# A layout turned on VectorE in place of DRAM, and a bias table written 16 times in place of 128

## The chip, the cores and the metric

The kernel runs on one core of one Trainium2 chip. The metric is the device time of one execution in microseconds (us); a figure for a kernel is the median of several executions. Engines: PE is TensorE (PEld its weight loads), DVE is VectorE, ACT is ScalarE, POOL is GpSimd, SP is SyncE, which here only issues DMAs.

## The reference

One sequence of 256 tokens of width 1024 runs in fp32 through a block (ffn1, a hybrid mixer, ffn2) and then through two layers (differential attention with an MLP, an mLSTM with an MLP). The change touches two small pieces of it.

In the mixer, each of 8 heads solves lower triangular systems of 64 rows, forward and backward in time:

```python
    a_mat = jnp.where(strict, jnp.einsum('bhnid,bhnjd->bhnij', k_beta, k) * decay, 0.0)
    a_mat = a_mat + jnp.eye(CHUNK, dtype=q.dtype)
    rhs = jnp.concatenate([v * beta[..., None], k_beta * jnp.exp(g)[..., None]], axis=-1)
    sol = lax.linalg.triangular_solve(a_mat, rhs, left_side=True, lower=True)
```

In attention, a bias is added that depends on the distance of query and key alone, one value per distance and head:

```python
        dist = (q0 + jnp.arange(Q_BLOCK))[:, None] - jnp.arange(kend)[None, :]
        bias = rel_table[t5_causal_bucket(jnp.maximum(dist, 0))]
        bias = jnp.transpose(bias, (2, 0, 1)).astype(jnp.float32)
        logits = jnp.einsum('bqhmd,bkhmd->bmhqk', qb, kb).astype(jnp.float32) * scale + bias
```

## The kernel before

**The main stream.** Every large product is done in units. A unit is 24 products of 128x128 weights with 128x256 activations: eight weight tiles, each as three products (L429, L430, L431), since fp32 weights and activations are split in a high and a low part (`whi`, `wlo`, `xh`, `xl`). Weights come as one long stream: SP issues DMAs of 1024 KB (L281, tile `raw`, three buffers), each of which feeds two units. ACT casts a unit's high part (L320, `whi`), DVE subtracts it for the low part (L323, `wlo`); this runs two units ahead of PE. PE therefore runs dry when a `raw` load lands late, or when DVE does not come round to `wlo`.

**The side work.** Everything small is written as generators in a list. `tick` steps each of them once per unit, before the unit's products are issued; a `yield` in such a generator is thus the distance of one unit, and the work after it stands one unit later in every engine's queue. All engines work strictly in the order so written. There is no planner: the place of a step is set by the count of `yield`s.

**`dn_inverse` (L1406)** is side work of the mixer's stage. It inverts the 32 diagonal blocks of 32x32 that the 64-row systems consist of on their diagonals, in place of solving row by row. The blocks are gathered as `c` (L1418 and L1424 on ACT, L1425 a transpose on DVE). The elimination (L1446, L1448: 31 steps on DVE, in groups between `yield`s) needs them as `m`, with rows and columns of each partition's 1024 elements exchanged across 32 partitions: `c` is written to DRAM (L1429) and read back by four strided DMAs (L1433). The result `x` goes the same way back: L1450 to DRAM, L1453 four reads into `xd`. Then `xt` is the transpose of `xd` (L1457 on DVE), and PE puts the 32-blocks together: 64 tiny products of 32x32 (L1464 to L1467), a copy on ACT (L1469, `t1`), 96 tiny products in one piece (L1474 to L1479), copies on POOL, DVE and ACT (L1481 to L1493), and after two more units products of 64x64 (L1503 and on).

**`bias_job` (L1009)** is side work of ffn2. One product (L1022) makes `brows`: 8 rows (one per head) of 384 distances. Attention wants them as `bias`, 128 partitions by 8 heads by 384, each partition shifted by one. A POOL DMA writes each row 128 times to DRAM (L1027, `bdram`, 1536 KB), and two POOL DMAs (L1030) read it back, their partition stride of 383 giving the shift. It is used in L1068, 145 us later.

Of the kernel before, what the change touches and what calls it, by code (L numbers as in the profile page):

```python
# [10 lines left out]
F32 = mybir.dt.float32  # L11
# [7 lines left out]
P = 128  # L19
D = 1024  # L20
S = 256
# [368 lines left out]
class Kern:  # L390
# [618 lines left out]
    def bias_job(self):  # L1009

        nc = self.nc
        es = ExitStack()
        self.bias = self.fin_attn.enter_context(self.tc.tile_pool(name="bias", bufs=1, side="right")).tile(
            [P, 8, S + P], F32, name="bias")
        keep2 = es.enter_context(self.tc.tile_pool(name="bias2", bufs=1, side="right"))
        rows = keep2.tile([8, 384], F32, name="brows")
        onehot = keep2.tile([P, 384], F32, name="onehot")
        nc.gpsimd.dma_start(onehot, self.arg["consts"][:, self.coff["onehot"][0]:])
        yield
        yield  # L1020
        ps = self.ps_up.tile([P, 384], F32, tag="up", name="up")
        nc.tensor.matmul(ps[:8], lhsT=self.vec("rel")[:33], rhs=onehot[:33], start=True, stop=True)  # L1022
        nc.scalar.copy(rows, ps[:8])
        yield

        d = self.dram.tile([8, P, 384], F32, name="bdram")
        nc.gpsimd.dma_start(d, rows.unsqueeze(1).to_broadcast([8, P, 384]))  # L1027
        yield
        for c, n in ((0, S), (P, P)):
            nc.gpsimd.dma_start(self.bias[:, :, c * 2:c * 2 + n],  # L1030
                                bass.AP(tensor=d.tensor, offset=d.offset + P - 1 + c, ap=[[383, P], [P * 384, 8], [1, n]]))
        yield
        es.close()

    def lambda_neg(self):
# [370 lines left out]
    def dn_inverse(self):  # L1406

        nc, m2, L = self.nc, self.m2, self.L
        v, t = nc.vector, nc.tensor
        four = lambda nm: m2.tile([P, 32, 32], F32, tag="inv", name=nm, bufs=3)  # L1410
        kh = lambda a: a.rearrange("p (k h) c -> p h k c", k=2)
        lf = lambda rows, cs: L[rows, :, 0:4:3, cs]
        lb = lambda rows, cs: L[rows, :, 4:6, cs]
        q = [slice(32 * s, 32 * s + 32) for s in range(4)]
        c = four("c")
        cf = m2.tile([P, 16, 32], F32, tag="inv2", name="cf", bufs=2)
        for s in range(4):
            nc.scalar.copy(kh(cf[q[s]]), lf(q[s], q[s]))  # L1418
        x = four("x")
        nc.gpsimd.memset(x, 0.0)  # L1420
        nc.gpsimd.memset(x.rearrange("p a b -> p (a b)")[:, 0:1024:33], 1.0)
        yield
        for s in range(4):
            nc.scalar.copy(kh(c[q[s], 16:]), lb(q[s], q[s]))  # L1424
        v.transpose(c[:, :16].rearrange("p a b -> p (a b)"), cf.rearrange("p a b -> p (a b)"))  # L1425
        yield
        d1 = self.dram.tile([P, 1024], F32, name="d1")
        d2 = self.dram.tile([P, 1024], F32, name="d2")
        nc.sync.dma_start(d1, c.rearrange("p a b -> p (a b)"))  # L1429
        m = four("m")  # L1430
        for s in range(4):

            nc.sync.dma_start(m[q[s]], d1[q[s]].rearrange("r (m c) -> m r c", m=32))  # L1433
        for _ in range(3):
            yield
        tmp = m2.tile([P, 256], F32, tag="tmp", name="tmp")
        done = 0
        for j in range(31):
            n, w = 31 - j, j + 1

            if done + n * w + 150 > 950:
                yield
                done = 0
            done += n * w + 150
            tt = tmp[:, :n * w].rearrange("p (a b) -> p a b", a=n)
            v.tensor_tensor(tt, m[:, j + 1:, j:j + 1].to_broadcast([P, n, w]),  # L1446
                            x[:, j:j + 1, :w].to_broadcast([P, n, w]), op=ALU.mult)
            v.tensor_sub(x[:, j + 1:, :w], x[:, j + 1:, :w], tt)  # L1448
        yield
        nc.sync.dma_start(d2, x.rearrange("p a b -> p (a b)"))  # L1450
        xd = four("xd")
        for s in range(4):
            nc.sync.dma_start(xd[q[s]], d2[q[s]].rearrange("m (r c) -> r m c", r=32))  # L1453
        for _ in range(2):
            yield
        xt = four("xt")
        v.transpose(xt.rearrange("p a b -> p (a b)"), xd.rearrange("p a b -> p (a b)"))  # L1457
        yield

        ix = lambda s, back: (s % 8, self.DIAG[s // 8 + 2 * back])  # L1460
        p = self.acc2().rearrange("p a (b c) -> p (a b) c", c=32)
        for s in range(16):
            f, b = ix(s, 0), ix(s, 1)
            t.matmul(p[q[1], s], lhsT=L[q[0], f[0], f[1], q[1]], rhs=xd[q[0], s], start=True, stop=True)  # L1464
            t.matmul(p[q[3], s], lhsT=L[q[2], f[0], f[1], q[3]], rhs=xd[q[2], s], start=True, stop=True)
            t.matmul(p[q[0], s], lhsT=L[q[1], b[0], b[1], q[0]], rhs=xt[q[1], 16 + s], start=True, stop=True)
            t.matmul(p[q[2], s], lhsT=L[q[3], b[0], b[1], q[2]], rhs=xt[q[3], 16 + s], start=True, stop=True)  # L1467
        t1 = m2.tile([P, 16, 32], F32, tag="inv2", name="t1", bufs=2)
        nc.scalar.copy(t1, p)  # L1469
        yield  # L1470
        p1 = self.acc2().rearrange("p a (b c) -> p (a b) c", c=32)
        p2 = self.acc2().rearrange("p a (b c) -> p (a b) c", c=32)
        for s in range(16):
            t.matmul(p1[q[0], s], lhsT=t1[q[1], s], rhs=xt[q[1], s], start=True, stop=True)  # L1474
            t.matmul(p1[q[2], s], lhsT=t1[q[3], s], rhs=xt[q[3], s], start=True, stop=True)
            t.matmul(p1[q[1], s], lhsT=t1[q[0], s], rhs=xd[q[0], 16 + s], start=True, stop=True)
            t.matmul(p1[q[3], s], lhsT=t1[q[2], s], rhs=xd[q[2], 16 + s], start=True, stop=True)
            t.matmul(p2[q[1], s], lhsT=xt[q[1], s], rhs=t1[q[1], s], start=True, stop=True)
            t.matmul(p2[q[2], s], lhsT=xd[q[2], 16 + s], rhs=t1[q[2], s], start=True, stop=True)  # L1479
        for s in range(4):  # L1480
            nc.gpsimd.tensor_copy(lf(q[s], q[s]), kh(xt[q[s], :16]))  # L1481
            nc.gpsimd.tensor_copy(lb(q[s], q[s]), kh(xd[q[s], 16:]))
        x64 = m2.tile([P, 16, 64], F32, tag="inv", name="x64", bufs=3)
        lo, hi = slice(0, 32), slice(32, 64)
        nc.vector.memset(x64, 0.0)
        for r, cc, src in ((0, lo, xd[q[0], :16]), (1, hi, xd[q[1], :16]), (2, lo, xt[q[2], 16:]), (3, hi, xt[q[3], 16:])):
            v.tensor_copy(x64[q[r], :, cc], src)
        v.tensor_scalar(x64[q[1], :, lo], p2[q[1]], -1.0, None, op0=ALU.mult)
        v.tensor_scalar(x64[q[2], :, hi], p2[q[2]], -1.0, None, op0=ALU.mult)
        nc.scalar.mul(lf(q[0], q[1]), kh(p1[q[0]]), -1.0)  # L1490
        nc.scalar.mul(lf(q[2], q[3]), kh(p1[q[2]]), -1.0)
        nc.scalar.mul(lb(q[1], q[0]), kh(p1[q[1]]), -1.0)
        nc.scalar.mul(lb(q[3], q[2]), kh(p1[q[3]]), -1.0)  # L1493
        yield
        yield

        u, w = slice(0, 64), slice(64, 128)
        t2 = m2.tile([P, 16, 64], F32, tag="inv", name="t2", bufs=3)
        for g in range(2):
            p = self.acc2().rearrange("p a (b c) -> p (a b) c", c=64)  # L1500
            for h in range(8):
                s = 8 * g + h
                t.matmul(p[w, h], lhsT=L[u, h, self.DIAG[g], w], rhs=x64[u, s], start=True, stop=True)  # L1503
                t.matmul(p[u, h], lhsT=L[w, h, self.DIAG[2 + g], u], rhs=x64[w, s], start=True, stop=True)
            nc.scalar.copy(t2[:, 8 * g:8 * g + 8], p)
        yield
        for g in range(2):
            f, b = self.DIAG[g], self.DIAG[2 + g]
            p = self.acc2().rearrange("p a (b c) -> p (a b) c", c=64)
            for h in range(8):  # L1510
                s = 8 * g + h
                t.matmul(p[u, h], lhsT=t2[w, s], rhs=L[w, h, f, w], start=True, stop=True)
                t.matmul(p[w, h], lhsT=t2[u, s], rhs=L[u, h, b, u], start=True, stop=True)
            nc.scalar.mul(L[u, :, f, w], p[u], -1.0)
            nc.scalar.mul(L[w, :, b, u], p[w], -1.0)
        yield
# [763 lines left out]
```

## Time and profile before

| what | value |
|---|---|
| time, median of 3 runs | 1355.5 us (1355.3 to 1356.18) |
| the profiled execution | 1354.97 us, its span 1353.2 us |
| mean granted clock of PE | 0.983 of full |
| PE busy | 1311.7 us, 97% of the span |
| DVE / ACT / POOL busy | 967.1 (71%) / 662.0 (49%) / 51.0 (4%) us |
| DMA moved | 259.99 MB, mean 192 GB/s |

The profiled execution lies 0.5 us below the median. PE's share is an average: it is busy nearly all the time, so what a change can bring lies in the few places where it is not, or where it runs at the lower of its clock levels (a product of 128x256 starts every 0.12 us at the full one, every 0.21 us at the half one). A matmul's own duration in the rows is longer than this distance, since successive ones overlap. In a row of the timeline, the brackets say how long the engine was idle before the instruction and what ended it.

### The profile page before, as it was taken

What the parts mean: (1) busy time and instruction counts of PE and PEld (TensorE: products, weight loads), DVE (VectorE), ACT (ScalarE), POOL (GpSimd) and SP (SyncE); (2) the same over time, 40 slices, a digit from 0 to 9 for tenths busy, and PEclk for the clock granted to TensorE, in tenths of its full rate; (3) what the DMA queues carried; (4) which work ended last, traced back from release to release, by engine and by line L of the source; (5) the groups of instructions that cost most, each with busy time, mean ns of one, the idle gap of its engine ahead of it and who ended that gap; (6) DMA issues with size and microseconds to landing.
All of it is one profiled execution on the core that took longest, in us unless ns stands there. A gap on an engine that the chain in (4) does not pass through costs nothing.

```text
span 1353.2 us, 26491 instructions
## 1 busy us (share of the span) xinstructions
PE 1311.7 (97%) x11090; PEld 1293.7 (96%) x11090; DVE 967.1 (71%) x1830; ACT 662.0 (49%) x1044; POOL 51.0 (4%) x36
## 2 busy tenths in 40 slices
PE   8999999999989999978999999999999999999997
PEld 7999999999979999978999999999999999999997
DVE  7997768789985587936446886876666957966664
ACT  3544445668434355614445555544444664644442
POOL 0000000343010000000000000000000000000000
PEclk8999999999989999988999999999999999999998
DMA  9898853444554365578554443455554435455550
GB/s 368 339 366 320 302 226 129 145 168 171 172 187 157 118 226 171 196 187 293 187 187 156 156 156 125 165 194 184 186 180 161 156 127 185 160 186 186 187 187 32
DMA packets 45912, 259.99 MB, mean 192 GB/s; under 512 B 12888, under 2 KB 13144, under 8 KB 15328
## 3 DMA queue, kind: packets, MB, share of 16 engines
q1 hardware_dynamic: 43744, 253.57, 53.3%
q0 software_dynamic: 1184, 3.35, 1.3%
q8 instruction: 87, 1.43, 0.4%
q10 hardware_dynamic: 864, 1.38, 0.3%
q14 instruction: 33, 0.27, 0.1%
HBM read 254.60 MB, written 3.67 MB: 191 GB/s over the span
## 4 chain that ended last, share of the span: by engine, by line
PE 84%; DVE 9%; DMA 3%; ACT 2%; issue 1%; SPq 0%; DVEq 0%; ACTq 0%
PE up L429 16%; PE up L431 15%; PE up L430 15%; PE acc L430 9%; PE acc L429 9%; PE acc L431 9%; DVE wlo L323 2%; DMA raw<-in_stream 2%; DVE raw L553 2%; PE acc L466 1%; PE acc L470 1%; PE acc L1297 1%; PE acc L1562 1%; PE acc L467 1%; PE acc L699 1%
## 5 line engine op out<-in xcount | busy, mean ns | idle before, releaser
L320 ACT CAST whi<-raw 128x1024 fp32r<-128x1024 f32 x404 | 420.4, 1047 | 434.7 <-PE up L430 166.5
L323 DVE TENSOR_TENSOR wlo<-raw,whi 128x1024 fp32r<-128x1024 f32 x389 | 472.5, 1223 | 79.4 <-ACT whi L320 77.5
L429 PE MATMUL up<-xh,whi 128*128 128x256 f32 x1744 | 503.5, 289 | 10.1 <-ACT whi L320 10.1
L431 PE MATMUL up<-xh,wlo 128*128 128x256 f32 x1744 | 497.9, 285 | 2.8 <-DVE wlo L323 2.8
L430 PE MATMUL up<-xl,whi 128*128 128x256 f32 x1744 | 497.3, 285 | 0.0
L429 PEld LDWEIGHTS up<-xh,whi 128*128 128x128 f32 x1744 | 338.8, 194 | 11.8 <-ACT whi L320 10.5
L431 PEld LDWEIGHTS up<-xh,wlo 128*128 128x128 f32 x1744 | 337.8, 194 | 4.5 <-DVE wlo L323 4.3
L430 PEld LDWEIGHTS up<-xl,whi 128*128 128x128 f32 x1744 | 337.9, 194 | 0.6 <-DVE xl L758 0.2
L429 PE MATMUL acc<-gh,whi 128*128 128x256 f32 x864 | 244.2, 283 | 0.0
L431 PE MATMUL acc<-gh,wlo 128*128 128x256 f32 x864 | 244.2, 283 | 0.0
L430 PE MATMUL acc<-gl,whi 128*128 128x256 f32 x864 | 244.1, 283 | 0.0
L429 PEld LDWEIGHTS acc<-gh,whi 128*128 128x128 f32 x864 | 166.0, 192 | 0.6 <-issue 0.6
L431 PEld LDWEIGHTS acc<-gh,wlo 128*128 128x128 f32 x864 | 164.7, 191 | 0.0
L430 PEld LDWEIGHTS acc<-gl,whi 128*128 128x128 f32 x864 | 164.7, 191 | 0.0
L991 DVE TENSOR_TENSOR t<-up,rs 128x256 f32<-128x256 f32 x60 | 25.4, 423 | 101.9 <-PE up L431 101.9
L553 DVE SCALAR_TENSOR_TENSOR raw<-raw,crow 128x1024 f32<-128x1024 f32 x72 | 85.7, 1218 | 3.3 <-DMA raw<-in_stream 3.3
L917 DVE TENSOR_TENSOR gf<-up,sa 128x256 f32<-128x256 f32 x35 | 14.5, 422 | 69.2 <-PE up L431 69.2
L323 POOL TENSOR_TENSOR wlo<-raw,whi 128x1024 fp32r<-128x1024 f32 x15 | 36.2, 2417 | 282.5 <-ACT whi L320 282.5
L429 PE MATMUL up<-whi,xh 128*128 128x256 f32 x128 | 37.3, 291 | 0.2 <-DVE raw L1933 0.2
L429 PE MATMUL acc<-yh,whi 128*128 128x256 f32 x128 | 36.3, 284 | 0.0
L913 ACT ACTIVATE sa<-up 128x256 f32<-128x256 f32 x35 | 13.2, 382 | 47.1 <-PE up L431 43.5
L430 PE MATMUL up<-wlo,xh 128*128 128x256 f32 x128 | 36.1, 282 | 0.0
(485 smaller groups left out, 1827.1 us busy)
## 6 DMA issues: line engine op xcount, KB each, us to landing
raw<-in_stream SPq DMA_DIRECT2D x238, 1024.0 KB, 5.0
bdram<-brows POOLq DMA_DIRECT2D x1, 1536.0 KB, 37.2
h<-in_x SPq DMA_DIRECT2D x2, 512.0 KB, 4.5
bias<-bdram POOLq DMA_DIRECT2D x1, 1024.0 KB, 10.4
d<-c SPq DMA_DIRECT2D x1, 512.0 KB, 2.6
m<-d SPq DMA_DIRECT2D x4, 128.0 KB, 4.0
d<-x SPq DMA_DIRECT2D x1, 512.0 KB, 5.6
xd<-d SPq DMA_DIRECT2D x4, 128.0 KB, 3.6
```

Source lines behind the costliest of these rows:

```text
L320: nc.scalar.copy(hi[:, :n], raw)
L323: self.lows.append(lambda: eng.tensor_tensor(lo[:, :n], raw, hi[:, :n].bitcast(F32), op=ALU.subtract))
L429: t.matmul(ps, lhsT=wh, rhs=xh, start=start, stop=False, skip_group_check=True)
L430: t.matmul(ps, lhsT=wh, rhs=xl, start=False, stop=False, skip_group_check=True)
L431: t.matmul(ps, lhsT=wl, rhs=xh, start=False, stop=stop, skip_group_check=True)
L466: t.matmul(ps, lhsT=wh[:, s], rhs=x[0][:, k], start=k == 0, stop=False, skip_group_check=True)
L467: t.matmul(ps, lhsT=wl[:, s], rhs=x[0][:, k], start=False, stop=False, skip_group_check=True)
L470: t.matmul(ps, lhsT=wh[:, s], rhs=x[1][:, k], start=False, stop=k == KT - 1, skip_group_check=True)
L553: self.nc.vector.scalar_tensor_tensor(w, w, 1.0, self.crow, op0=ALU.mult, op1=ALU.mult, accum_out=self.mods[:, c:c + 1])
L699: self.nc.tensor.matmul(ps[:, c0 + b * P:c0 + (b + 1) * P], lhsT=tok[:, b:b + 1].to_broadcast([P, P]), rhs=self.const("ident"), start=True ...
L917: product(n, lambda gf: None, lambda gf: nc.vector.tensor_tensor(gf, ps, sa, op=ALU.mult))
L991: nc.vector.tensor_tensor(t, src, self.rs, op=ALU.mult)
```

## The change

Three edits.

1. In `dn_inverse` the two trips through DRAM go (two writes and eight reads on SP's queue). In their place DVE transposes 32x32 blocks with strided views: `m` from `c` and `xd` from `x`, each of 128x1024 elements. The three `yield`s behind the first trip become one, the two behind the second become one; the limit that closes a group of elimination steps goes from 950 to 900, which makes 14 groups of 13.
2. The 96 tiny products are cut in two halves of 48 by a `yield`, so that a unit's 24 products stand between them.
3. In `bias_job` each row goes to DRAM 16 times in place of 128 (192 KB). Eight reads of 16 partitions each (128 KB), two per `yield`, make `bias[:, :, :256]`; three `yield`s later POOL copies the last 128 columns, which equal columns 128 to 255.

```diff
-        d = self.dram.tile([8, P, 384], F32, name="bdram")
-        nc.gpsimd.dma_start(d, rows.unsqueeze(1).to_broadcast([8, P, 384]))
-        yield
-        for c, n in ((0, S), (P, P)):
-            nc.gpsimd.dma_start(self.bias[:, :, c * 2:c * 2 + n],
-                                bass.AP(tensor=d.tensor, offset=d.offset + P - 1 + c, ap=[[383, P], [P * 384, 8], [1, n]]))
-        yield
+        d = self.dram.tile([8, 16, 384], F32, name="bdram")
+        nc.gpsimd.dma_start(d, rows.unsqueeze(1).to_broadcast([8, 16, 384]))
+        yield
+        for q in range(0, P, 16):
+            nc.gpsimd.dma_start(self.bias[q:q + 16, :, :S],
+                                bass.AP(tensor=d.tensor, offset=d.offset + P - 1 - q, ap=[[383, 16], [16 * 384, 8], [1, S]]))
+            if q % 32:
+                yield
+        for _ in range(3):
+            yield
+        nc.gpsimd.tensor_copy(self.bias[:, :, S:], self.bias[:, :, P:S])
         es.close()
...
-        d1 = self.dram.tile([P, 1024], F32, name="d1")
-        d2 = self.dram.tile([P, 1024], F32, name="d2")
-        nc.sync.dma_start(d1, c.rearrange("p a b -> p (a b)"))
         m = four("m")
-        for s in range(4):
-
-            nc.sync.dma_start(m[q[s]], d1[q[s]].rearrange("r (m c) -> m r c", m=32))
-        for _ in range(3):
-            yield
+
+        v.transpose(m.rearrange("p r c -> p c r"), c.rearrange("p m c -> p c m"))
+        yield
...
-            if done + n * w + 150 > 950:
+            if done + n * w + 150 > 900:
...
-        nc.sync.dma_start(d2, x.rearrange("p a b -> p (a b)"))
         xd = four("xd")
-        for s in range(4):
-            nc.sync.dma_start(xd[q[s]], d2[q[s]].rearrange("m (r c) -> r m c", r=32))
-        for _ in range(2):
-            yield
+        v.transpose(xd.rearrange("p m c -> p c m"), x.rearrange("p r c -> p c r"))
+        yield
...
             t.matmul(p2[q[2], s], lhsT=xd[q[2], 16 + s], rhs=t1[q[2], s], start=True, stop=True)
+            if s == 7:
+                yield
```

Counting `yield`s from the transpose of `c` to the first tiny product gives 20 before and 18 after: this product stands two units earlier in PE's queue.

On DVE, at the end of the inverse, the queue reads so before (from the last elimination step; `ct`, `cy`, `cb`, `yal` are the convolution branch of the mixer, `wlo` the stream):

```order
L1446 TENSOR_TENSOR tmp<-m,x 128x31
L1448 TENSOR_TENSOR x<-x,tmp 128x31
L323 TENSOR_TENSOR wlo<-raw,whi 128x1024
L1738 SCALAR_TENSOR_TENSOR cy<-ct,vecs,cy 128x255
L1740 SCALAR_TENSOR_TENSOR cy<-ct,vecs,cy 128x255
L1742 TENSOR_TENSOR cb<-cb,cy 128x256
L323 TENSOR_TENSOR wlo<-raw,whi 128x1024
L1734 TENSOR_TENSOR ct<-up,cc 128x256
L323 TENSOR_TENSOR wlo<-raw,whi 128x1024
L489 TENSOR_TENSOR yal<-cb,yah 128x256
L1457 STREAM_TRANSPOSE xt<-xd 128x1024
```

And so after, from the same step (line numbers are those of the changed kernel; L1445 and L1447 are the elimination, L1450 the new transpose, L1453 the old one):

```order
L1445 TENSOR_TENSOR tmp<-m,x 128x31
L1447 TENSOR_TENSOR x<-x,tmp 128x31
L1732 TENSOR_TENSOR ct<-up,cc 128x256
L323 TENSOR_TENSOR wlo<-raw,whi 128x1024
L489 TENSOR_TENSOR yal<-cb,yah 128x256
L1450 STREAM_TRANSPOSE xd<-x 128x32x32
L323 TENSOR_TENSOR wlo<-raw,whi 128x1024
L1736 SCALAR_TENSOR_TENSOR cy<-ct,vecs,cy 128x255
L1738 SCALAR_TENSOR_TENSOR cy<-ct,vecs,cy 128x255
L1740 TENSOR_TENSOR cb<-cb,cy 128x256
L1453 STREAM_TRANSPOSE xt<-xd 128x1024
```

The elimination ends earlier against the stream's work (the first `ct`, `wlo`, `yal` now come behind it), and the transpose to `xt` stands directly behind the convolution's `cb`, where two more `wlo` stood ahead of it before.

On PE, the middle of the second group of tiny products before, at the place where half of them are issued:

```order
L1478 MATMUL acc<-t_4882,xt 32x32
L1479 MATMUL acc<-t_4882,xd 32x32
L1474 MATMUL acc<-xt,t_4882 32x32
L1475 MATMUL acc<-xt,t_4882 32x32
L1476 MATMUL acc<-xd,t_4882 32x32
L1477 MATMUL acc<-xd,t_4882 32x32
```

And the same place after (L1474 and L1475 are the last two of the first half):

```order
L1474 MATMUL acc<-t_4802,xt 32x32
L1475 MATMUL acc<-t_4802,xd 32x32
L429 MATMUL up<-xh,whi 128x256
L430 MATMUL up<-xl,whi 128x256
L431 MATMUL up<-xh,wlo 128x256
```

A whole unit of 24 products follows there, and the other 48 tiny products come behind it.

On POOL, around the bias table before (the onehot table's load first, the next stage's first work last):

```order
L1018 DMA onehot<-in_consts 128x384
L1027 DMA bdram<-brows 1024x1x384
L1030 DMA bias<-bdram 128x8x256
L1030 DMA bias<-bdram 128x8x128
L1885 TENSOR_TENSOR sq<-sq 128x2x256 x2
```

And after:

```order
L1018 DMA onehot<-in_consts 128x384
L1027 DMA bdram<-brows 128x1x384
L1030 DMA bias<-bdram 16x8x256 x8
L1036 COPY bias<-bias 128x8x128
L1883 TENSOR_TENSOR sq<-sq 128x2x256 x2
```

The write is an eighth of what it was, the reads are eight small ones, and one copy takes the place of the second read; nothing else of POOL's moves.

## Rows read from the trace of the kernel before

**Rows 1.** the chain that ended last, shares of the span by engine (page)

```profile
PE 84%; DVE 9%; DMA 3%; ACT 2%; issue 1%; SPq 0%; DVEq 0%; ACTq 0%
```

**Rows 2.** PE's waits over the run: waited for, total us, times, longest

```profile
PE up L429 <- ACT whi L320: 10.1, 2, 6.3
...
PE acc L1465 <- DMA xd<-d: 1.9, 1, 1.9
```

**Rows 3.** PE's timeline in the mixer: start us, us, instruction [idle before]

```profile
393.47 0.28 PE L430 MATMUL up<-xl,whi 128*128 128x256 f32 x1
393.59 0.28 PE L431 MATMUL up<-xh,wlo 128*128 128x256 f32 x1
...
399.43 0.26 PE L1466 MATMUL acc<-xt,L 32*32 32x32 f32 x1 [1.71 <-DVE xt L1457]
...
401.28 0.58 PE L429 MATMUL up<-xh,whi 128*128 128x256 f32 x1
...
406.14 0.28 PE L431 MATMUL up<-xh,wlo 128*128 128x256 f32 x1
...
410.49 0.21 PE L1476 MATMUL acc<-xd,t 32*32 32x32 f32 x1 [2.39 <-issue]
```

**Rows 4.** two windows there; PEclk is third from the right

```profile
400.00:405.00 5.00, 5.00 (x117) 4.94 (x107) 4.77 (x6) 0.58 (x1) 4.92 (x6) 0.50 0.65 223
...
410.00:415.00 5.00, 4.51 (x43) 4.47 (x44) 2.45 (x4) 3.57 (x6) 0.00 (x0) 1.00 0.02 3
```

**Rows 5.** DVE's timeline from the first `wlo` behind `c` to `xt`

```profile
336.44 0.41 DVE L1302 TENSOR_TENSOR Pm<-acc,Pm 128x256 f32<-128x256 f32 x1
...
343.61 1.23 DVE L323 TENSOR_TENSOR wlo<-raw,whi 128x1024 fp32r<-128x1024 f32 x1 [1.96 <-ACT whi L320]
...
347.05 0.20 DVE L1446 TENSOR_TENSOR tmp<-m,x 128x31 f32<-128x31 f32 x1
...
386.48 0.19 DVE L1446 TENSOR_TENSOR tmp<-m,x 128x31 f32<-128x31 f32 x1
...
388.98 0.43 DVE L1742 TENSOR_TENSOR cb<-cb,cy 128x256 f32<-128x256 f32 x1
...
398.13 1.25 DVE L1457 STREAM_TRANSPOSE xt<-xd 128x1024 f32<-128x1024 f32 x1 [5.14 <-DMA xd<-d]
```

**Rows 6.** PE's timeline in ffn2

```profile
594.05 0.28 PE L431 MATMUL acc<-gh,wlo 128*128 128x256 f32 x1
600.64 0.58 PE L429 MATMUL up<-xh,whi 128*128 128x256 f32 x1 [6.32 <-ACT whi L320]
...
613.82 0.39 PE L429 MATMUL up<-xh,whi 128*128 128x256 f32 x1 [3.81 <-ACT whi L320]
...
620.97 0.28 PE L431 MATMUL up<-xh,wlo 128*128 128x256 f32 x1
```

**Rows 7.** DMA issues: KB each, median us to landing (page)

```profile
raw<-in_stream SPq DMA_DIRECT2D x238, 1024.0 KB, 5.0
bdram<-brows POOLq DMA_DIRECT2D x1, 1536.0 KB, 37.2
...
bias<-bdram POOLq DMA_DIRECT2D x1, 1024.0 KB, 10.4
...
m<-d SPq DMA_DIRECT2D x4, 128.0 KB, 4.0
```

**Rows 8.** POOL's timeline in ffn2

```profile
574.80 1.11 POOL L1027 DMA_DIRECT2D bdram<-brows  x1 [8.85 <-ACT brows L1023]
```

**Rows 9.** DMA, 585 to 590 us: queue shares of 16 engines, issues

```profile
q0 software_dynamic: 52, 0.24, 48.0%
...
raw<-in_stream SPq DMA_DIRECT2D x1, 1024.0 KB, 25.8
```

**Rows 10.** DMA, 615 to 620 us: queue shares, issues

```profile
raw<-in_stream SPq DMA_DIRECT2D x2, 1024.0 KB, 8.5
```

**Rows 11.** POOL on 128x1024: busy us, mean ns of one (page)

```profile
L323 POOL TENSOR_TENSOR wlo<-raw,whi 128x1024 fp32r<-128x1024 f32 x15 | 36.2, 2417 | 282.5 <-ACT whi L320 282.5
```

## The prediction

> **What bounds the kernel now.** I read the chain of waits first: 84% of it is PE [rows 1], so time is lost where PE waits or runs slowly, and almost nowhere else. The list of PE's waits then gives the places. The largest entry, 10.1 us in two waits for ACT's casts of weights, is in ffn2. A wait of 1.9 us for `xd`, the inverse's second trip through DRAM, stands in the mixer [rows 2]. Last I read the timelines of PE around both places. In the mixer PE's last product starts at 393.59 and the first group of tiny products, after a wait for `xt` of 1.71 us more, gets going at 399.43; the unit behind it crawls from 401.28 to 406.14; and in the middle of the 96 tiny products PE sits 2.39 us with nothing to wait for that the profile shows ("issue") [rows 3]. In ffn2 PE stands for 6.32 and 3.81 us, and the products between run at the wide distance [rows 6].
>
> **The bias table.** The write of 1536 KB takes 37.2 us to land [rows 7]. While it runs, its queue holds 48.0% of the 16 engines' time though it moves only 0.24 MB in 5 us, and a weight load takes 25.8 us in place of 5.0 [rows 7, 9]. The write is issued at 574.8 [rows 8]; the raw buffers cover it up to PE's last product at 594.05, 19.25 us [rows 6]; then ACT has nothing to cast and PE stands. What this costs comes from the first and the last of the disturbed products: from 594.05 to 620.97 there are 78 of them, which at full speed need 78 x 0.12 = 9.36 us, so 26.92 - 9.36 = 17.56 us are lost [rows 3, 6]. Of these 10.13 are the two waits; most of the rest is PE at half clock behind them.
>
> The change writes an eighth. At the same rate that is 37.2 / 8 = 4.65 us, a quarter of the stretch that the buffers cover. If it takes twice that, the cover still holds. The eight reads are bounded from below by the reads of before: 1536 KB in two DMAs, 10.4 us for the larger [rows 7], beside which weight loads took 8.5 us [rows 10]. A load feeds two units, 48 products or 5.76 us, and three are in flight, so 8.5 us starve nobody. From above, the nearest row of this size is `m<-d`, 128 KB in 4.0 us [rows 7]: two reads in one unit's time are then no more traffic than before, spread over four units. I take the whole loss as gone but for half a microsecond: gain 17.0, between 14 (one late load left) and 17.56. POOL's copy of 128x1024 elements costs at most 2.4 us by its subtraction of that size [rows 11]; PE and ACT do not wait for it, as attention needs the table over 100 us later. That distance covers the longer `bias_job` as well.
>
> **The inverse: what DVE now carries.** The trips through DRAM leave SP's queue, where weight loads stood behind them; two transposes go to DVE. Before, DVE worked from 336.44 nearly without a gap: one wait of 1.96 us at 343.61, and at 389.33 its last `cb` is done (start 388.98 plus 0.35 until the next instruction) [rows 5]. That is 52.9 - 1.96 = 50.9 us of work. The new order puts the same work ahead of `xt`, plus the two transposes of T us each; since the elimination starts two units earlier, its first steps fill that gap. So `xt` starts at 336.44 + 50.9 + 2T = 387.3 + 2T.
>
> T is not in the trace. Contiguous, a transpose of 128x1024 takes 1.25 us [rows 5]; from below there is no reason for less. For strided access the elimination shows something: its first step walks 31 elements 128 bytes apart and takes 0.20 us, its last 31 side by side in 0.19 [rows 5]. If the 0.01 us is all due to the stride it makes 0.33 us per 1024, so T = 1.6; if the whole 0.20 grew with the elements, T = 6.6, the far end. I take 1.25 to 1.6, since the row says that the stride costs next to nothing, and sum with 1.25.
>
> [...]
>
> With T = 1.25 `xt` starts at 389.8, ends at 391.05, and tiny products start at 391.1. Before they started at 399.43, but two units (2 x 2.88 = 5.76 us) later in PE's order: 393.67 on the same footing. Gain 2.55. PE itself would be there at 393.71 - 5.76 = 387.95, so a wait of about 3 us stays, and DVE is what PE waits for; part of it will show as late `wlo` in the units ahead.
>
> **Clock.** Behind these waits the granted clock is 0.50 [rows 4], the lower of the two levels, and the unit takes 4.86 us, where 23 distances of 0.12 are 2.76: 2.1 lost [rows 3]. Behind the pause of 2.39 us the clock is 1.00 [rows 3, 4]; behind one of 3.81 PE crawls again (620.97 - 613.82 is 7.15 us) [rows 6]. A wait of 3 us in two or three pieces lies nearer the first. I take the 2.1 as gained; the other end is 0.
>
> **The halves.** The 2.39 us pause [rows 3] comes after most of the 96 tiny products, each with its own weight load, have gone in one run, and nothing that the profile shows is waited for: I read it as PE running out of fetched instructions. With 48 products, then a unit of 2.9 us, then 48, I expect the pause to go; gain 2.4, or 0 if the supply needs longer. The 64x64 products behind stand no nearer to the last tiny ones than before, so no wait is added there.
>
> **Sum.** Inverse 2.55 + 2.1 + 2.4 = 7.05, bias 17.0, together 24.0. On the profiled execution: 1354.97 - 24.0 = 1331.0; it lies 0.5 below the median of the runs, so by the median 1331.5. I say 1331. The main case's own range goes down to 1325.5: 17.56, with 5.7 + 2.1 + 2.4 in the mixer if PE never stands there, makes 1327.2, and 1.7 more are for clock and waits elsewhere. It goes up to 1334, where the pause is kept.
>
> **Rivals.**
> 1. DVE becomes the bound in the inverse. With T = 2.5, twice the contiguous row, `xt` starts at 392.3, PE at 393.6, the gain there is nothing, PE stands 5.6 us and the clock falls as before: the mixer gives 2.4 or nothing. Time 1354.97 - 17.0 - 2.4 = 1335.6, or 1338 with the pause kept. At T = 6.6 PE starts at 401.8, 8.1 us are lost there, and the time is 1344 to 1346. For it: DVE had one gap of 1.96 us in this stretch of 53. Against: the 0.20 beside 0.19. Chance 0.18.
> 2. The narrow reads hold the engines as the write did. At the write's rate (1536 KB in 37.2 us, 41 KB/us) 1024 KB last 24.8 us, 29.4 with the write. Of the write's 37.2 us the last 17.9, behind the cover of 19.25, carried the loss of 17.56; 29.4 leave 10.2 us behind the cover, so 10 us of loss: gain 7.6 in place of 17.0, time 1340.3. For it: the rate fits a transfer with 8 partitions on one side, and these reads have 16. Against: `m<-d`, 32 partitions wide, does 128 KB in 4.0 us [rows 7]. Chance 0.10. [...]
> 3. The slower side: each small read takes as long as the large one, 10.4 us, one after the other, with weight loads at 25.8 us all the while. That is 83 + 4.65 us, 68.6 behind the cover; at 17.56 lost per 17.9 us it costs 67 us in place of 17.56, so 1354.97 + 49.5 - 7.05 = 1397. It eats up the mixer's gain from 44 us in all, 5.0 us per read in a row. For it: the reads go out on the queue that delayed the loads. Against: beside the reads of before loads took 8.5 us, not 25.8 [rows 10]. Chance 0.04.
> 4. The write does not shrink: it still reads 8 partitions, and if a fixed part, not the bytes, makes its 37.2 us, then only the mixer's 7.05 are left: 1348. Chance 0.04.
>
> **Chances and range.** The main case has 0.64. A measurement of this kernel can tell about 0.2%, 2.7 us. All cases but the third are faster by more: 0.95 faster, 0.01 the same, 0.04 slower. From 1325.5 to 1341 the range takes in the main case, rival 1 up to T near 5, and rival 2; left out are 3, 4 and the tails.
>
> **What would show it.** Right: the waits for `xd` gone and the one at the first tiny product for DVE's transpose, 3 us or less, at most 4 with the `wlo` before it; strided transposes of 1.2 to 1.6 us; granted clock near 1.00 from 395 to 410; no "issue" wait in either half; `bdram` landing in 4 to 8 us; weight loads under 10 us in ffn2; no wait of PE for a cast there. Wrong: a strided transpose above 2 us; a pause in the tiny products still there; weight loads over 15 us beside the eight reads; or a new place at which PE stands for POOL or DVE in ffn2.

## The result, and the profile after

The changed kernel takes 1339.5 us (median; 1337.6 to 1340.4), the kernel before 1355.4 on the same chip: a ratio of 0.9883, 95% interval 0.9866 to 0.9901. That is 16 us less, faster as forecast, but two thirds of the 24 us that the sum gave (1331). It lies in the stated range of 1325.5 to 1341, but above the 1334 at which the main case's own part of it ends.

To see where the time went I lined the two traces up product by product: both have 9456 products of the main stream (L429 to L431), and the n-th of one is the n-th of the other. The difference of their start times, before less after, in us:

```
product                          before at   difference
2304  ahead of the inverse          325.4        0.25
3048  behind the mixer's solve      476.6        6.36
3900  ahead of the disturbed ffn2   587.0        6.54
4200  behind it                     640.4       16.10
9432  end                          1337.3       15.78
```

So the mixer gives 6.1 (7.05 forecast) and ffn2 gives 9.7 (17.0 forecast). Nearly all of the missing time is in ffn2.

PE's waits of the changed kernel (waited for: total us, times, longest) answer to [rows 2]:

```profile
PE up L429 <- ACT whi L320: 5.0, 1, 5.0
...
PE acc L1462 <- DVE xt L1453: 2.5, 1, 2.5
...
PE acc L1301 <- ACT V L1396: 1.1, 1, 1.1
```

The waits for `xd` are gone, and one of 2.5 us for DVE's transpose stands in their place. One of the two waits for casts in ffn2 is still there, with 5.0 us. A small new one, 1.1 us for `V`, at 339.6 us, stands in every kernel that has the edits to the inverse and in neither of the two without them. DVE's timeline after, which answers to [rows 5]:

```profile
336.20 2.13 DVE L1433 STREAM_TRANSPOSE m<-c 128x1024 f32<-128x1024 f32 x1
...
386.66 2.25 DVE L1450 STREAM_TRANSPOSE xd<-x 128x1024 f32<-128x1024 f32 x1
...
391.27 1.24 DVE L1453 STREAM_TRANSPOSE xt<-xd 128x1024 f32<-128x1024 f32 x1
```

The strided transposes take 2.13 and 2.25 us, near the first rival's 2.5 and not the 1.25 of the sum. Hence `xt` comes at 392.5, and on PE (to compare with [rows 3]):

```profile
389.91 0.19 PE L1461 MATMUL acc<-xd,L 32*32 32x32 f32 x1
392.57 0.26 PE L1462 MATMUL acc<-xt,L 32*32 32x32 f32 x1 [2.46 <-DVE xt L1453]
...
394.41 0.58 PE L429 MATMUL up<-xh,whi 128*128 128x256 f32 x1
...
395.63 0.28 PE L431 MATMUL up<-xh,wlo 128*128 128x256 f32 x1
...
397.77 0.28 PE L431 MATMUL up<-xh,wlo 128*128 128x256 f32 x1
```

The unit behind crawls for five products only (394.41 to 395.63), then runs at full distance; it takes 3.36 us, not 4.86. No "issue" row appears. The granted clock (third from the right) in windows after, the first behind the new wait for `V`, the others behind that for `xt`:

```profile
340.00:345.00 5.00, 5.00 (x29) 4.92 (x28) 4.73 (x15) 0.05 (x2) 0.00 (x0) 0.66 0.65 210
...
390.00:395.00 5.00, 2.54 (x130) 2.37 (x127) 3.55 (x5) 2.15 (x4) 2.31 (x3) 0.72 0.25 66
395.00:400.00 5.00, 5.00 (x128) 4.83 (x128) 1.84 (x4) 1.57 (x3) 3.18 (x6) 0.94 0.48 197
```

Behind the wait for `xt` it is 0.72 and 0.94, where before it fell to 0.50 [rows 4]; from 340 to 345 us it is 0.66, where the kernel before had 1.00.

In ffn2, POOL's timeline (the write, the eight reads, the copy) and PE's, to compare with [rows 6, 8]:

```profile
570.49 0.63 POOL L1027 DMA_DIRECT2D bdram<-brows  x1 [11.06 <-ACT brows L1023]
576.41 4.20 POOL L1030 DMA_DIRECT2D bias<-bdram  x8 [5.29 <-DMA bdram<-brows]
596.96 1.04 POOL L1036 COPY bias<-bias 128x1024 f32<-128x1024 f32 x1 [16.35 <-DMA bias<-bdram]
```

```profile
593.22 0.28 PE L431 MATMUL up<-xh,wlo 128*128 128x256 f32 x1
598.50 0.58 PE L429 MATMUL up<-xh,whi 128*128 128x256 f32 x1 [5.00 <-ACT whi L320]
...
603.90 0.29 PE L429 MATMUL up<-xh,whi 128*128 128x256 f32 x1
```

The write lands within 5.9 us: it has shrunk as forecast. But the reads last from 576.4 to 597.0, twenty microseconds for 1 MB, and at their end PE stands. From 593.22 to 603.90 there are 22 products, so 10.68 - 22 x 0.12 = 8.0 us are lost; 17.56 - 8.0 = 9.5 is what ffn2 gained, near the 9.7 of the lined-up traces.

Two windows show the difference between the old reads and the new. The DMA of the kernel before while its wide reads ran, 612 to 627 us (queue: packets, MB, share of the 16 engines; then the issues):

```profile
q1 hardware_dynamic: 532, 3.88, 65.0%
q0 software_dynamic: 416, 1.57, 31.3%
...
raw<-in_stream SPq DMA_DIRECT2D x3, 1024.0 KB, 8.5
```

And of the changed kernel while its narrow reads run, 577 to 598 us:

```profile
q1 hardware_dynamic: 510, 3.74, 75.1%
q0 software_dynamic: 384, 1.05, 24.6%
...
raw<-in_stream SPq DMA_DIRECT2D x4, 1024.0 KB, 13.5
bias<-bdram POOLq DMA_DIRECT2D x7, 128.0 KB, 11.9
```

The engines are full in both, but the weights (q1) get 3.88 MB in 65.0% of 16 x 15 us, 24.9 KB per engine and us, before, and 3.74 MB in 75.1% of 16 x 21, 14.8 KB, after. While the narrow reads are about, the weight packets are slow as well (0.54 us for one of 8 KB, median, in place of 0.31), and a weight load takes 13.5 us where it took 8.5.

### The profile page after: what moved, and what is told of

Its sections match the earlier page's. It is cut to its first block, busy times and chain, and to the rows that moved or that the text cites. A ratio compares the mean times of both kernels' runs of the same rounds, so it can differ in the third digit from the quotient of the medians.

```text
span 1337.5 us, 26486 instructions
## 1 busy us (share of the span) xinstructions
PE 1305.4 (98%) x11090; PEld 1288.1 (96%) x11090; DVE 969.2 (72%) x1832; ACT 661.3 (49%) x1044; POOL 52.4 (4%) x43
## 3 DMA queue, kind: packets, MB, share of 16 engines
HBM read 253.03 MB, written 1.25 MB: 190 GB/s over the span
## 4 chain that ended last, share of the span: by engine, by line
PE 86%; DVE 9%; DMA 2%; ACT 2%; issue 1%; SPq 0%; DVEq 0%; ACTq 0%
PE up L429 16%; PE up L431 16%; PE up L430 16%; PE acc L430 9%; PE acc L429 9%; PE acc L431 9%; DVE wlo L323 2%; DVE raw L553 2%; DMA raw<-in_stream 1%; PE acc L699 1%; PE acc L1301 1%; PE acc L1560 1%; PE acc L466 1%; PE acc L470 1%; PE acc L467 1%
## 5 line engine op out<-in xcount | busy, mean ns | idle before, releaser
L429 PE MATMUL up<-xh,whi 128*128 128x256 f32 x1744 | 501.5, 288 | 5.0 <-ACT whi L320 5.0
L431 PE MATMUL up<-xh,wlo 128*128 128x256 f32 x1744 | 495.4, 284 | 1.8 <-DVE wlo L323 1.8
L429 PEld LDWEIGHTS up<-xh,whi 128*128 128x128 f32 x1744 | 336.9, 193 | 6.5 <-ACT whi L320 5.2
L431 PEld LDWEIGHTS up<-xh,wlo 128*128 128x128 f32 x1744 | 335.6, 192 | 2.9 <-DVE wlo L323 2.7
L429 PE MATMUL acc<-gh,whi 128*128 128x256 f32 x864 | 244.3, 283 | 0.0
L431 PE MATMUL acc<-gh,wlo 128*128 128x256 f32 x864 | 244.3, 283 | 0.0
L429 PEld LDWEIGHTS acc<-gh,whi 128*128 128x128 f32 x864 | 166.1, 192 | 0.6 <-issue 0.6
L431 PEld LDWEIGHTS acc<-gh,wlo 128*128 128x128 f32 x864 | 164.7, 191 | 0.0
L429 PE MATMUL up<-whi,xh 128*128 128x256 f32 x128 | 37.3, 292 | 0.2 <-DVE raw L1931 0.2
L429 PE MATMUL acc<-yh,whi 128*128 128x256 f32 x128 | 36.3, 284 | 0.0
```

Source lines behind the costliest of these rows:

```text
L429: t.matmul(ps, lhsT=wh, rhs=xh, start=start, stop=False, skip_group_check=True)
L431: t.matmul(ps, lhsT=wl, rhs=xh, start=False, stop=stop, skip_group_check=True)
```

## The experiments

All times are medians; ratios are to the kernel before on the same chip.

| run | time | ratio, 95% interval | mixer, ffn2 (lined up, us gained) |
|---|---|---|---|
| changed kernel | 1339.5 | 0.9883 (0.9866 to 0.9901) | 6.1, 9.7 |
| bias_alone | 1344.9 | 0.9922 (0.9903 to 0.9941) | 0.1, 10.1 |
| inverse_alone | 1350.3 | 0.9963 (0.9948 to 0.9977) | 3.4, 1.7 |
| comb_reads | 1335.4 | 0.9848 (0.9832 to 0.9863) | 4.8, 15.5 |
| transpose_prices | 1340.8 | one run | 4.2, 10.2 |
| reads_on_sp | 1333.7 | 0.9832 (0.9813 to 0.9850) | 4.2, 17.5 |
| rows_128 | 1362.1 | one run | 4.1, -9.1 |
| heads_128 | 1350.2 | one run | 4.8, -0.3 |
| no_cut | 1342.0 | one run | 4.5, 9.0 |
| one_unit_more | 1339.5 | 0.9873 (0.9859 to 0.9888) | 4.9, 9.6 |
| xt_early | 1332.9 | 0.9812 (0.9791 to 0.9832) | 5.6, 16.5 |
| three_cuts | 1330.9 | 0.9811 (0.9791 to 0.9832) | 7.6, 16.7 |

The last column is of one profiled execution each, products 2304 to 3048 and 3048 to 4200. It carries some 1.5 us that I take for chance: in the solve behind the inverse the granted clock falls for a few us in most of these executions, at changing places (455 to 460 us: 0.66 in comb_reads; 465 to 470: 0.77 before), and in those of the changed kernel and of bias_alone it does not. That it is chance is not shown, since each kernel has one trace; the mean clock of one kernel's executions does differ, 0.986 to 0.988 in the changed kernel.

**Do the parts add up?** bias_alone puts the third edit of the diff into the kernel before; inverse_alone leaves it out of the changed one.

> The kernel before with the bias edit alone. Lined up product by product, the changed kernel's traces give 9.4 us to ffn2 and 6.1 to the mixer. Theory: the two parts do not touch each other, so this kernel is 9.4 us faster than before: about 1346. The eight reads land in about 11 us each and weight loads beside them in 13 to 16, with one wait of PE for a cast of about 5 us. Rival: the weight loads of ffn2 are late only because the shorter mixer shifts them against the reads; then this kernel has no such wait and is 16 to 17 us faster, about 1339.

> The kernel before with the edits to the inverse alone (transposes, 900, the two halves). Theory, parts independent: 6.1 us faster than before, about 1349, with the strided transposes at 2.1 to 2.3 us, a wait of 2.5 us for the transpose to xt, no pause in the tiny products, and ffn2 losing the 17.6 us of before. Rival: the mixer's gain is taken back in ffn2, where the long write starves PE by the weights' place in the queue; then less than 3 us faster.

They gave 10.6 us (1 - 0.9922 of 1355) and 5.0 us, together 15.6 against 15.9 for both. Each of these is good to 2 or 3 us; as far as that shows, the parts do not touch each other, and the rivals fall. bias_alone's waits and inverse_alone's:

```profile
PE up L429 <- ACT whi L320: 3.9, 2, 3.7
...
PE acc L1480 <- issue: 2.5, 1, 2.5
```

```profile
PE up L429 <- ACT whi L320: 9.7, 2, 6.1
...
PE acc L1458 <- DVE xt L1449: 2.5, 1, 2.5
```

With the bias edit alone the wait for a cast remains (3.9), and the pause of the inverse as well; with the inverse alone the 9.7 of the long write remain.

**Neighbours or the source?** The eight reads of the changed kernel, with the partitions of each 8 apart (`comb[q]` is partitions q, q + 8, ..., q + 120 of `bias`):

```diff
-            nc.gpsimd.dma_start(self.bias[q:q + 16, :, :S],
-                                bass.AP(tensor=d.tensor, offset=d.offset + P - 1 - q, ap=[[383, 16], [16 * 384, 8], [1, S]]))
+            nc.gpsimd.dma_start(comb[q, :, :, :S],
+                                bass.AP(tensor=d.tensor, offset=d.offset + P - 1 - q, ap=[[376, 16], [16 * 384, 8], [1, S]]))
```

> The changed kernel, but each of the eight reads fills 16 partitions that lie 8 apart in place of 16 neighbours; same write, same 16 rows of DRAM, same bytes, count and places of the DMAs. Theory N: 16 neighbouring partitions are what is slow; spread over all 128, the reads land in 3 to 6 us, weight loads beside them in under 9, PE does not wait for a cast, and the time falls by about 7.7 us to 1332. Rival S: the source (16 rows of 1.5 KB read by eight DMAs) or the small DMAs themselves are slow; then reads stay near 11 us, the wait of 5 us stays and the time is 1339 to 1340.

In between. PE's wait for the cast fell from 5.0 to 1.0 us, and the time to 1335.4; but the reads land in 9.6 us, not 3 to 6. The weights' queue in the window 577 to 590:

```profile
q1 hardware_dynamic: 319, 2.35, 65.3%
```

The weights get 2.35 MB in 65.3% of 16 x 13 us, 17.3 KB per engine and us: between 14.8 and 24.9. So which partitions a read fills matters, with source and size the same; it is not all.

**Distinct rows, then whole width.** rows_128 writes each row 128 times again and gives the narrow reads the distinct rows that the wide reads had; heads_128 reads the same bytes in eight DMAs of the same 128 KB, but each over all 128 partitions for one head.

```diff
 rows_128:
...
+            nc.gpsimd.dma_start(self.bias[q:q + 16, :, :S],
+                                bass.AP(tensor=d.tensor, offset=d.offset + P - 1 + 383 * q, ap=[[383, 16], [P * 384, 8], [1, S]]))
 heads_128:
...
+            nc.gpsimd.dma_start(self.bias[:, q, :S],
+                                bass.AP(tensor=d.tensor, offset=d.offset + P - 1 + P * 384 * q, ap=[[383, P], [1, S]]))
```

> The changed kernel, but each row is written 128 times as before and the eight reads of 16 neighbouring partitions take distinct rows, as the wide reads of before did. The long write costs its 17 us again, so the time is about 1350; what counts is the stretch of the reads. Theory S (16 rows shared by all reads are the slow source): reads land in under 8 us and the weight loads beside them in about 8.5, as beside the wide reads of before. Theory D (the small narrow DMAs themselves are slow): reads stay at 10 us or more, and loads beside them at 11 to 15.

> As rows_128 (each row written 128 times, eight reads of 128 KB, two per unit, on POOL's queue), but each read fills all 128 partitions for one head, in place of 16 partitions for eight heads. Theory W (what is slow is that a read fills few partitions): reads land in under 8 us, weight loads beside them in about 8.5, and the third wait of PE for a cast, 4.8 us in rows_128, is gone; time 1352 to 1354. Theory C (eight small reads are slow by their count and size): reads stay over 10 us, loads at 11 or more, the third wait stays, time about 1362.

The stretch of the reads in rows_128, 609 to 629 us, and in heads_128, 609 to 620:

```profile
q1 hardware_dynamic: 440, 3.23, 66.4%
q0 software_dynamic: 375, 1.03, 35.1%
...
raw<-in_stream SPq DMA_DIRECT2D x3, 1024.0 KB, 13.8
bias<-bdram POOLq DMA_DIRECT2D x8, 128.0 KB, 16.8
```

```profile
q1 hardware_dynamic: 388, 2.85, 66.5%
q0 software_dynamic: 384, 1.05, 31.0%
...
raw<-in_stream SPq DMA_DIRECT2D x3, 1024.0 KB, 6.7
bias<-bdram POOLq DMA_DIRECT2D x8, 128.0 KB, 6.0
```

This settles it between the source and the width. With distinct rows the narrow reads are no better (16.8 us, worse even), so the 16 shared rows were not the fault. With the same source, bytes, count and queue, only the width differs between the two, and with it which rows one DMA takes: 4.26 MB in 20 us against 3.90 MB in 11, and for the weights 15.2 KB per engine and us against 24.4. PE's waits for casts, of rows_128 and then heads_128:

```profile
PE up L429 <- ACT whi L320: 16.1, 3, 7.6
```

```profile
PE up L429 <- ACT whi L320: 12.4, 2, 8.3
```

The third is gone, and the time is 12 us lower, in single runs; 8.8 of the 12 lie in ffn2. (rows_128 was expected at about 1350, and missed that by 12.) So a read on this queue that fills 16 partitions holds the engines, and the weights with them: these got 14.8 KB per engine and us beside 16 neighbours, 17.3 beside the comb, 24.4 beside 128. Why this is so, and why the comb costs less than neighbours, no run shows. In the changed kernel, beside the weight loads, 1.05 MB took the 20.6 us from the first issue to POOL's copy, 51 GB/s, and no run shows the reads alone.

**Another queue.** reads_on_sp issues the same narrow reads from SP, between the weight loads, three units after the write.

```diff
+        for _ in range(3):
+            yield
         for q in range(0, P, 16):
-            nc.gpsimd.dma_start(self.bias[q:q + 16, :, :S],
+            nc.sync.dma_start(self.bias[q:q + 16, :, :S],
```

> The changed kernel with its eight reads issued by SP, in the weights' own queue, three units after the write. Theory Q (two queues that take turns on the same 16 engines are slow): each read lands in 3 to 5 us as m<-d did, weight loads near them in under 8, no wait of PE for a cast, time 1331 to 1333. Theory S (these 16 rows are a slow source, whoever asks): reads and the loads behind them stay slow, at 10 us or more, a wait of some us stays, time 1336 to 1340.

1333.7 us, and no wait of PE for a cast in the whole run: ffn2 gave 17.5, all of the 17.56. Window 577 to 598 (the reads are on q1 here):

```profile
q1 hardware_dynamic: 1504, 5.75, 93.8%
...
raw<-in_stream SPq DMA_DIRECT2D x5, 1024.0 KB, 8.0
bias<-bdram SPq DMA_DIRECT2D x8, 128.0 KB, 9.9
```

The time is near what theory Q had, the landing is not: a read takes 9.9 us from issue, not 3 to 5; it shares its queue with five weight loads. What is gained is that one after the other they move 5.75 MB in 21 us, where two queues at once moved 4.79 (3.74 + 1.05). Narrow reads still cost, but they no longer slow the weight packets beside them: a weight packet of 8 KB takes 0.31 us here (median), as beside the wide reads of before, and 0.54 in the changed kernel's window. With the queue the edit changed two things more, the reads' packets (1 KB in place of 4) and their time (three units later); no run parts these from the queue.

**The price of a stride.** transpose_prices adds eight transposes on a scratch tile:

```diff
+        for ki, ko in ((1, 1), (2, 1), (4, 1), (32, 1), (1, 2), (1, 4), (1, 32), (32, 32)):
+            nc.vector.transpose(tb.rearrange("p (a b) -> p b a", b=ko), ta.rearrange("p (a b) -> p b a", b=ki))
+            yield
```

> The changed kernel with eight transposes of 128x1024 added in ffn2, one per unit, on a scratch tile: reading with a step of 1, 2, 4 and 32 elements and writing side by side, then writing with a step of 2, 4 and 32, then 32 on both sides. Theory L (a price for every element that lies on another 16-byte line): step 2 as step 1 (1.25 us), steps 4 and 32 alike and dearer, near 2.2. Theory B: only the strided writing, or only both together, is dear; then three or more of the strided forms stay at 1.25 and the last is 2.2. By either the time is a few us above the changed kernel's.

In that order (reading steps 1, 2, 4, 32 elements; writing steps 2, 4, 32; both 32):

```profile
610.62 1.24 DVE L1043 STREAM_TRANSPOSE pb<-pa 128x1024 f32<-128x1024 f32 x1
...
613.22 1.23 DVE L1043 STREAM_TRANSPOSE pb<-pa 128x1024 f32<-128x1024 f32 x1
...
615.81 2.09 DVE L1043 STREAM_TRANSPOSE pb<-pa 128x1024 f32<-128x1024 f32 x1
...
618.92 2.09 DVE L1043 STREAM_TRANSPOSE pb<-pa 128x1024 f32<-128x1024 f32 x1
...
622.03 1.25 DVE L1043 STREAM_TRANSPOSE pb<-pa 128x1024 f32<-128x1024 f32 x1
...
624.62 2.07 DVE L1043 STREAM_TRANSPOSE pb<-pa 128x1024 f32<-128x1024 f32 x1
...
627.97 2.07 DVE L1043 STREAM_TRANSPOSE pb<-pa 128x1024 f32<-128x1024 f32 x1
...
631.33 2.24 DVE L1043 STREAM_TRANSPOSE pb<-pa 128x1024 f32<-128x1024 f32 x1
```

The prices are as theory L had them: a step of 2 (8 bytes) is free (1.23 us reading, 1.25 writing, beside 1.24), 4 (16 bytes) costs 0.85 us, 32 no more than 4, reading or writing alike (2.09 and 2.07 us), and both together only 0.15 more (2.24). Of the reason that theory L gives, a line of 16 bytes, the run shows no more than that the price comes between steps of 8 and of 16 bytes. Both sides of the kernel's own transposes are strided, by 32 elements, and they took 2.13 and 2.25 us.

**The pause in the tiny products.** no_cut takes the `yield` between the two halves out; one_unit_more puts one more `yield` behind the transpose to `xt`.

```diff
 no_cut:
-            if s == 7:
-                yield
 one_unit_more:
         v.transpose(xt.rearrange("p a b -> p (a b)"), xd.rearrange("p a b -> p (a b)"))
         yield
+        yield
```

> The changed kernel without the yield that cuts the 96 tiny products. Theory I (PE runs out of fetched instructions when 96 products with their loads go in one run): a pause of 2 to 2.5 us before one of the last products comes back, nothing else moves, time 1341 to 1342. Rival: the pause of before was an after-effect of the waits on DRAM; then no pause, and the time is that of the changed kernel.

> The changed kernel with one more yield behind the transpose to xt, so that PE does a unit of 2.9 us there. Theory: DVE's lateness at this one place is all that PE waits for; the wait of 2.5 us and the half clock behind it go, 3 to 3.7 us in all, and the time is 1336. Rival: DVE is the bound of the whole stretch; then the wait shows up again at a wlo or at the 64x64 products, and the time stays within 1 us of the changed kernel.

Theory I, as it was put, falls. In no_cut the 96 products go in one run without a pause; its mixer gains 4.5 us, as much as the kernels that share the rest of it (4.1 to 4.8 in comb_reads, rows_128 and heads_128). Its 1342.0, a single run, lies in the range of theory I, but not by a pause. And one_unit_more, with the cut in place, has a pause:

```profile
PE acc L1473 <- issue: 1.7, 1, 1.7
```

Its wait for `xt` is gone as expected, but the pause and the clock that falls behind it (0.75 from 405 to 410 us) take the gain back: 1339.5, as before the edit. So the cut is not what removed the pause.

The traces show what did. On the page of the kernel before, PE's records and the queue of instructions:

```profile
PE 1311.7 (97%) x11090; PEld 1293.7 (96%) x11090; DVE 967.1 (71%) x1830; ACT 662.0 (49%) x1044; POOL 51.0 (4%) x36
...
q8 instruction: 87, 1.43, 0.4%
```

Its 87 packets of 16 KB go with PE's 22180 records (weight loads and products), 255 to a packet. Counted from the start of the run, every pause lies ahead of record 6811, or of record 6299, which is 2 x 256 earlier, and ends 1.3 to 1.5 us after a packet of this queue has landed:

| kernel | pause ahead of record | packet, from and to (us) | PE goes on (us) |
|---|---|---|---|
| before | 6811 | 407.86, 409.17 | 410.49 |
| bias_alone | 6811 | 407.80, 408.72 | 410.21 |
| one_unit_more | 6811 | 401.62, 402.56 | 403.81 |
| xt_early (below) | 6299 | 390.61, 391.55 | 393.00 |

The packet of the first row in its window, 407.8 to 409.2 us:

```profile
q8 instruction: 1, 0.02, 5.9%
```

From this I take it that PE did run out of fetched instructions, and that what counts is how fast it gets through one block of 256 records. In the kernel before, the block ahead of 6811 lies wholly in the 96 tiny products (each stands in the trace as two products and two weight loads, so 384 records) and lasts 1.27 us (406.83 to the pause at 408.10); the next packet set out 1.0 us after its start. In the changed kernel and in no_cut the tiny products stand two units, 96 records, earlier, so that main products share the block: 5.0 and 5.9 us, and no pause. In one_unit_more, where they stand only one unit earlier, the block lasts 4.3 us, but the packet set out 3.7 us after its start; why so late, no run shows.

**A better version.** xt_early (on top of reads_on_sp) makes `xt` straight behind `xd`, with both `yield`s after it. three_cuts (on top of that) also cuts the first 64 tiny products in two.

```diff
 xt_early:
         v.transpose(xd.rearrange("p m c -> p c m"), x.rearrange("p r c -> p c r"))
-        yield
         xt = four("xt")
         v.transpose(xt.rearrange("p a b -> p (a b)"), xd.rearrange("p a b -> p (a b)"))
         yield
+        yield
 three_cuts, in the loop of the first group:
             t.matmul(p[q[2], s], lhsT=L[q[3], b[0], b[1], q[2]], rhs=xt[q[3], 16 + s], start=True, stop=True)
+            if s == 7:
+                yield
```

> reads_on_sp, and in addition xt is made straight behind xd on DVE, ahead of a wlo and the convolution's three operations, with both yields behind it, so PE's order is unchanged. Theory: the wait of 2.5 us for xt falls to under 0.5, with the half clock behind it; 3 us less than reads_on_sp if nothing takes its place, 1330 to 1331. Rival, from one_unit_more: the wait was what gave PE's instruction supply time, so an issue pause of 1.5 to 2.5 us comes in the tiny products, and the time stays within 1 us of reads_on_sp (1333 to 1334.5).

> xt_early, and the first group of 64 tiny products is cut in two halves of 32 as well, with a unit between. Theory I2 (the tiny groups use up instructions faster than they are fetched, wherever the fetch happens to stand; more units between give it time): the pause of 1.29 us with the half clock behind it goes and no other comes, 1.5 to 3 us less than xt_early, 1330 to 1331.5. Rival: the pause only moves to another place of the same stretch; then the time stays within 1 us of xt_early's 1332.9.

In xt_early the wait went and a pause came, this time in the unit behind the first group, ahead of record 6299 (in the kernels with the wait of 2.5 us for `xt`, that wait lies in the block of 256 before this record):

```profile
393.00 0.36 PE L430 MATMUL up<-xl,whi 128*128 128x256 f32 x1 [1.29 <-issue]
```

Its time is 0.9 us under reads_on_sp, inside what the intervals leave open: the rival's case. In three_cuts there is no pause and no crawl; windows of it:

```profile
390.00:395.00 5.00, 4.86 (x154) 4.29 (x152) 4.93 (x6) 2.25 (x4) 4.32 (x5) 1.00 0.18 72
395.00:400.00 5.00, 5.00 (x147) 4.78 (x135) 4.96 (x7) 2.83 (x5) 4.65 (x4) 1.00 0.61 215
```

PE is busy for 9.86 of these 10 us at full clock, and the mixer gains 7.6 us, the most of all runs, 2.0 over xt_early. The median, 1330.9, lies in theory I2's range and is the lowest; the ratio (0.9811) does not differ from xt_early's (0.9812), so on the whole time that gain is not shown, on the trace it is. Both beat the changed kernel: 0.981 against 0.9883, some 9.7 us, most of which reads_on_sp (0.9832) had.

## Why the prediction came out as it did

- **The range:** it held (1339.5 in 1325.5 to 1341), but by the room that it gave to the rivals; the main case alone ended at 1334.
- **What bounds the kernel:** right. The two places held all of the change; bias_alone and inverse_alone add up to it.
- **The write:** right. An eighth of the bytes, landing within 5.9 us (4.65 forecast), inside the cover.
- **The reads: the step that failed.** "From above, the nearest row of this size is `m<-d`, 128 KB in 4.0 us" took a price by its size alone. That row is a load of 32 partitions on SP's queue; these are 16 partitions on POOL's, beside full weight traffic. They took 11.0 us and made the weight loads 13.5, not "8.5 us starve nobody". The term was 17.0 and measured 9.7. The second rival had the place and about the time (1340.3), and its doubt was right: it spoke for 16 partitions on one side. It was set aside with the same wrong row. heads_128 and rows_128 show the width as the cause on POOL's queue, reads_on_sp that the term was to be had whole.
- **T, the strided transpose: mis-sized.** 1.25 taken, 2.13 and 2.25 measured. The elimination's 0.20 beside 0.19 us could not tell: 0.85 us per 1024 elements, as measured, is 0.026 for its 31, a difference that rounding hides. So the gain at the first tiny product was 393.67 - 392.57 = 1.1, not 2.55. The rest of DVE's path was right: 387.3 + 2.13 + 2.25 = 391.7, and `xt` started at 391.27. That DVE is what PE then waits for was right too, but that the wait came out near its size (2.46 us, "about 3" forecast) is luck: `xt` came 1.5 us later than in the sum (392.57, not 391.1), and PE was there 2.2 us later (390.1, not 387.95), most of which is the wait for `V` and the low clock behind it.
- **Clock:** right in kind. The crawl shrank from 4.86 to 3.36 us for the unit, so 1.5 of the 2.1 came.
- **The halves:** the pause went in this kernel, 2.4 us, and the traces of the four kernels with a pause agree with the reading that PE ran out of fetched instructions: PE goes on 1.3 to 1.5 us after a packet of them has landed. But the cut did not do it (no_cut has none either): the products' place, two units earlier, did, which the prediction did not count for this. The gain of this term is luck.
- **Sum of the mixer:** 1.1 + 1.5 + 2.4 = 5.0. The new wait for `V` takes nothing from it, since PE waits for `xt` behind it anyway; the lined-up 6.1 has in it the fall of the clock in the solve (some 1.5 us) that the execution before had and this one did not. inverse_alone's 5.0 us, over several runs, agrees with the sum.

## What to carry to other kernels

Price a DMA by the partitions it fills and by what runs beside it on which queue, not by its bytes: fewer bytes written were paid for with narrow reads beside which a weight load took 13.5 us in place of 8.5, and moving the reads into the weights' own queue (8.0 us) got it back. For a strided operation, a row of a few elements cannot bound the price per element; look for a long one, or price the strided form in a run of its own (1.24 us side by side, 2.24 with a step of 32 elements on both sides). Where many tiny products go in a row, count PE's records: in the kernel before, a block of 256 that held nothing else was used up in 1.27 us, while the next packet landed 2.3 us after its start.

## What the runs showed of the hardware beyond this

- In rows_128 and heads_128 eight DMAs of 128 KB from the same rows, on the same queue, land in 16.8 us where each fills 16 partitions, and in 6.0 us where each fills 128.
- A transpose of 128x1024 takes 1.24 us with a step of 4 or 8 bytes, 0.85 us more with one of 16 or 128 bytes on either side, and only 0.15 on top of that for 128 bytes on both.
- PE's pause with nothing to wait for (2.39, 2.5, 1.7 and 1.29 us in four kernels; none in the nine others, with the same products) stands each time at the end of a block of 256 of PE's records. In all thirteen kernels the first record of such a block started 1.26 us or more after the packet of 16 KB that goes with it had landed. 256 records of the main stream last 15 us (128 products, 0.12 us each), of 32x32 products 1.27 us.
